# The first overflow job of a mixture-of-experts stage: its search and its loads moved into the fifth of eight passes

## The chip, the core and the metric

The kernel runs on one core of a Trainium2 chip. The core has a matrix engine (TensorE, PE in the profile), two engines for element-wise work that matter here (VectorE, DVE; ScalarE, ACT), a third one (GpSimd, POOL), and SyncE (SP), which in this kernel issues nearly all loads from device memory. ScalarE issues some loads too. Each engine takes its own instructions in the order in which they stand, and waits on semaphores for the others. The metric is the time of one execution in device microseconds, as the median over several runs.

## What is computed

Two blocks follow each other on 256 tokens of width 1024: a block with two attentions and a feed-forward network, and then two layers of the second kind, each with an attention, a mixture of experts and a gated per-layer embedding. The change is in the mixture of experts, once in each of the two layers (layer 0 and layer 1):

```
def hier_moe(xn, w_group, b_group, w_expert, b_expert, w_gate, w_up, w_down):
...
    e_w, e_idx = lax.top_k(e_prob, TOPK_IN_GROUP)
    e_w = e_w / jnp.sum(e_w, axis=-1, keepdims=True)
    comb = g_w * e_w
    expert_id = g_idx * EXPERTS_PER_GROUP + e_idx
    cw = jnp.einsum('tk,tke->te', comb, jax.nn.one_hot(expert_id, N_EXPERTS, dtype=jnp.float32)).astype(xt.dtype)
    hid = jax.nn.silu(jnp.einsum('td,edf->tef', xt, w_gate)) * jnp.einsum('td,edf->tef', xt, w_up)
    y = jnp.einsum('tef,efd->td', hid * cw[:, :, None], w_down)
```

There are 32 experts of width 128 in 4 groups; a token goes to two experts of one group. All is float32.

## The kernel before

The kernel computes an expert only for the tokens that chose it. It runs eight passes (`for q in range(8)`, L1129; the fifth has q = 4), each for four experts, and gives every expert 32 places (`CAP`). A pass runs, on PE: the gate and up matmuls of its four experts side by side (`gate_up`, L1021, L1027), the products of the pass before added into four accumulators (`combine`, L1054, L1058), a transpose of the hidden values (`turn`, L1038, L1040), the gather of tokens for later passes (`gather`, L983, L995) with the transposes of their choice (`slots`, L1008), and the down projection (`down`, L1043, L1047). Between them ScalarE and VectorE do the activation (`hidden`, L1032: tanh at L1034, then L1035 and L1036) and move results out of the accumulators (L1005, L1002, L1051, L1052). `turn` stands in PE's queue right behind `combine` and waits for the hidden values.

The weights of a pass are six tiles of 1 MB (four with gate and up of one expert, two with the down weights of two). A `Stream` takes them from a list and issues their loads on SyncE (L320, L328) into an arena of 21 tiles, as far ahead as `W.room(peak)` allows: at most 21 - peak tiles are held. The stage has `W.room(2)`, and from the sixth pass on `W.room(4)` in layer 1 and `W.room(9)` in layer 0.

An expert with more than 32 tokens is a job more. `jobs` (L953 to L957) counts these for each expert, `njob_i` is their number. They are run behind the last pass, by `overflow` (L1064): all engines read the number from memory into a register (L1068), skip the body if it is zero, and else run a loop. One trip of it loads a table of places (`place`, L1076), finds an expert with tokens left (L1078 to L1093), reads its number into a register of ScalarE (L1082), loads its three weights from there (L1084, L1085), makes the matrix that picks its tokens (L1095, L1096), gathers (L1104, whose matmuls are L995 too), and runs gate, up and down for up to 112 tokens (L1107 to L1124). Behind the branch comes the last pass's own `combine(T, True)` (L1177), and with it the end of the stage.

PE's and SyncE's instructions stand in the order of the code; those of the other engines are put in order by a scheduler.

Of the kernel before, what the change touches and what calls it, by code (L numbers as in the profile page):

```python
# [10 lines left out]
F32 = mybir.dt.float32  # L11
# [10 lines left out]
S = 256  # L22
# [229 lines left out]
def block_kernel(ctx, tc, I, out):  # L252
# [615 lines left out]
    def moe(l, router, rs):  # L868
# [195 lines left out]
        def overflow(T):  # L1064

            gu, dn = take("ovg", [2, 1024]), take("ovd", [1024])
            R = Step(new_d(128), T)
            n = nc.values_load(njob_i[0:1, 0:1], min_val=0, max_val=32)  # L1068
            with tc.If(n > 0):
                with tc.For_i(0, n, 1):  # L1070
                    tmp = sq2("job")
                    key, hot, cwh = tmp[:, 0:32], tmp[:, 32:64], tmp[:, 64:128].rearrange("p (t q e) -> p t q e", t=2, q=8)
                    top, cnt, keyj = tmp[:, 128:129], tmp[:, 129:130], tmp[:, 130:134].rearrange("p (t a) -> p t a", t=2)
                    wj, place, ei = tmp[:, 134:138].rearrange("p (t a) -> p t a", t=2), tmp[:, 256:384], tmp[:, 138:139]
                    wr = new_d(4)
                    nc.scalar.dma_start(place, I["c_place"])  # L1076
                    ebase = C("ebase")[:, 0:32]
                    V.tensor_scalar(key, ebase, float(S), None, OP.add)  # L1078
                    V.scalar_tensor_tensor(hot, jobs, 0.5, key, OP.is_gt, OP.mult)
                    V.tensor_reduce(top, hot, AX.X, OP.max)  # L1080
                    V.tensor_scalar(ei.bitcast(I32), top, 1.0 / S, -1.0, OP.mult, OP.add)
                    e = nc.values_load(ei.bitcast(I32)[0:1, 0:1], engines=(ENG.Activation,), min_val=0, max_val=31)  # L1082
                    for a, src in enumerate((I["moe_w_gate_2"], I["moe_w_up_2"])):
                        nc.scalar.dma_start(gu[:, a].unsqueeze(1), src[l, bass.ds(e, 1)].rearrange("e (p k) f -> p e (k f)", k=8))  # L1084
                    nc.scalar.dma_start(dn.unsqueeze(1), I["moe_w_down_2"][l, bass.ds(e, 1)].rearrange("e p n -> p e n"))  # L1085
                    V.tensor_scalar(hot, key, top, None, OP.is_equal)
                    V.tensor_tensor(key, jobs, hot, OP.mult)
                    V.tensor_reduce(cnt, key, AX.X, OP.add)
                    V.tensor_tensor(jobs, jobs, hot, OP.subtract)

                    V.tensor_scalar(cnt, cnt, float(MORE), float(CAP - MORE + 1 - S), OP.mult, OP.add)
                    V.tensor_tensor(cnt, cnt, top, OP.add)
                    V.tensor_scalar(keyj, k8[:, :, 0:2], cnt, None, OP.subtract)  # L1093
                    for t in range(2):
                        V.tensor_scalar(R.d[:, t], place, keyj[:, t, 0:1], None, OP.is_equal)  # L1095
                        V.scalar_tensor_tensor(R.d[:, t], place, keyj[:, t, 1:2], R.d[:, t].bitcast(F32),  # L1096
                                               OP.is_equal, OP.add)
                    for t in range(2):
                        V.tensor_tensor(cwh[:, t], cw[:, t, :, 0:4], hot.rearrange("p (q e) -> p q e", q=8), OP.mult)
                        V.tensor_reduce(wj[:, t, 0:1], cwh[:, t].rearrange("p q e -> p (q e)"), AX.X, OP.add)  # L1100
                        V.tensor_copy(wj[:, t, 1:2], cw[:, t, 0, 4:5])
                    A.copy(wr[:, :, 0:2], wj)
                    V.tensor_tensor(wr[:, :, 2:4], wj, wr[:, :, 0:2].bitcast(F32), OP.subtract)
                    drain(gather(R.d, [R], R.banks))  # L1104
                    b = R.bank("ex")
                    for t in range(2):
                        nc.tensor.transpose(b[:, t * 128:(t + 1) * 128], R.d[:, t].bitcast(F32), ident)  # L1107
                    for t in range(2):
                        mm(b[:, 256:260], R.d[:, t], wr[:, t], start=t == 0, stop=t == 1)
                    A.copy(R.d, b[:, 0:256].rearrange("p (t n) -> p t n", t=2))  # L1110
                    A.copy(R.ej[:, 0], b[:, 256:260])
                    V.tensor_tensor(R.cs, R.ej[:, 0, 0:2], R.ej[:, 0, 2:4], OP.add)
                    V.tensor_scalar(R.cs[:, 0:1], R.cs[:, 0:1], 0.5, None, OP.mult)
                    b = R.gu()
                    for k in range(8):
                        mm(b[:, 0:256], R.xe[:, k], gu[:, :, k * 128:(k + 1) * 128], start=k == 0, stop=k == 7)
                    hidden(R)
                    turn(R)
                    for c in range(2):
                        b = R.bank(f"y{c}")  # L1120
# [8 lines left out]
        for q in range(8):  # L1129
# [9 lines left out]
            if q == 2:  # L1139
                pv_ = ple_load(l)  # L1140
            if q == 5:
                W.room(4 if l else 9)
# [902 lines left out]
```

## Time and profile before

| | us |
|---|---|
| median of 3 runs | 880.39 (879.73 to 885.22) |
| the profiled execution | 883.1 |
| its span, first to last instruction | 881.3 |
| PE busy in the span | 829.3 (94%) |
| VectorE, ScalarE, GpSimd busy | 512.2, 453.0, 225.0 |
| mean granted clock of TensorE | 0.971 of full speed |

The rows below are from this one execution; times in them are microseconds from its first instruction unless marked ns. "ACTq" and "SPq" are the queues on which ScalarE and SyncE issue; a DMA row there gives the issue, not the transfer. The number in brackets is how long the engine idled before the instruction and whose work ended that. PEclk is the granted clock, where 1.00 is 2.4 GHz and 0.50 is 1.2 GHz. Matmul ends are modelled, so a row's length is that of a row of overlapping matmuls. In layer 0 the stage runs from about 484 to 626, in layer 1 from about 745 to 849.

### The profile page before, as it was taken

Reading aid. Unit: us, or ns where it says so; the run is one execution under the profiler, and the core shown is the slowest. Engines: PE = TensorE matmul, PEld = TensorE weight load, DVE = VectorE, ACT = ScalarE, POOL = GpSimd, SP = SyncE. Lnnn points to the kernel's source line nnn. Section 1 sums busy time; section 2 is a strip of 40 time slices with the busy share of each in tenths; the row PEclk is TensorE's granted clock in tenths of the full one; section 3 lists DMA queues with packets and bytes.
Section 4 is the critical chain, followed back from the end, with each engine's and each line's share of the span. In section 5 each row is a group of like instructions: output and inputs, shape, how many; then the busy total and the mean of one; then the engine's idle time right before and its main releaser. Section 6 shows DMA issues by size and latency. Waiting matters only on the chain. (4 is left out here: it accounts for less than half of the span.)

```text
span 881.3 us, 15729 instructions
## 1 busy us (share of the span) xinstructions
PE 829.3 (94%) x5660; PEld 647.4 (73%) x5660; DVE 512.2 (58%) x1479; ACT 453.0 (51%) x1106; POOL 225.0 (26%) x293
## 2 busy tenths in 40 slices
PE   8997999999999999999899999965899899999997
PEld 5995878999999988686667666635587778666656
DVE  5669656755454567678664544321688765543355
ACT  6675875544444456267675133420666774232463
POOL 2225542322222234214453200000122355000011
PEclk9998999999999999999799999995999899999999
DMA  9990429655556542446015699999463515799961
GB/s 307 385 375 31 146 81 399 237 191 171 198 179 188 182 144 96 161 141 237 1 50 197 254 378 406 408 397 379 157 207 129 208 66 193 293 384 406 408 262 49
DMA packets 85137, 200.05 MB, mean 227 GB/s; under 512 B 5776, under 2 KB 27584, under 8 KB 85056
## 3 DMA queue, kind: packets, MB, share of 16 engines
q1 hardware_dynamic: 82704, 195.61, 61.1%
q10 hardware_dynamic: 2352, 3.40, 1.1%
q8 instruction: 46, 0.75, 0.3%
q14 instruction: 35, 0.29, 0.1%
HBM read 197.93 MB, written 1.06 MB: 226 GB/s over the span
## 5 line engine op out<-in xcount | busy, mean ns | idle before, releaser
L537 DVE TENSOR_TENSOR s<-a,s 128x512 fp32r<-128x512 f32 (+3 forms) x281 | 189.5, 685 | 121.7 <-ACT s L536 87.0
L536 ACT CAST s<-a 128x512 fp32r<-128x512 f32 (+3 forms) x294 | 172.6, 600 | 169.8 <-PE pj L543 71.7
L541 PE MATMUL pj<-s,a 128*128 128x512 f32 (+3 forms) x456 | 176.1, 386 | 4.6 <-ACT a L518 3.0
L542 PE MATMUL pj<-s,a 128*128 128x512 f32 (+3 forms) x456 | 170.5, 374 | 5.9 <-DVE s L537 5.8
L543 PE MATMUL pj<-s,a 128*128 128x512 f32 (+3 forms) x456 | 170.4, 374 | 1.3 <-DVE a L519 1.2
L537 POOL TENSOR_TENSOR s<-a,s 128x512 fp32r<-128x512 f32 (+3 forms) x71 | 90.1, 1269 | 304.6 <-ACT s L536 246.6
L541 PEld LDWEIGHTS pj<-s,a 128*128 128x128 f32 x456 | 86.4, 190 | 24.1 <-issue 5.6
L534 POOL TENSOR_SCALAR s<-a 128x512 fp32r<-128x512 f32 (+3 forms) x58 | 40.3, 696 | 242.3 <-PE pj L543 113.9
L542 PEld LDWEIGHTS pj<-s,a 128*128 128x128 f32 x456 | 86.7, 190 | 20.1 <-DVE s L537 7.8
L543 PEld LDWEIGHTS pj<-s,a 128*128 128x128 f32 x456 | 86.6, 190 | 18.2 <-DVE a L519 3.6
L1517 PE MATMUL f<-a,s 128*128 128x256 f32 x256 | 72.6, 284 | 0.0
L1519 PE MATMUL f<-a,s 128*128 128x256 f32 x256 | 72.4, 283 | 0.0
L1518 PE MATMUL f<-a,s 128*128 128x256 f32 x256 | 72.4, 283 | 0.0
L1027 PE MATMUL gu<-a,xe 128*32 128x256 f32 x1024 | 58.7, 380 | 0.7 <-DVE xe L1002 0.7
L1027 PEld LDWEIGHTS gu<-a,xe 128*32 128x32 f32 x1024 | 32.5, 110 | 28.4 <-issue 4.9
L541 PE MATMUL acc<-s,a 128*128 128x512 f32 x128 | 50.1, 391 | 0.0
L542 PE MATMUL acc<-s,a 128*128 128x512 f32 x128 | 49.9, 390 | 0.0
L543 PE MATMUL acc<-s,a 128*128 128x512 f32 x128 | 49.8, 389 | 0.0
L1518 PEld LDWEIGHTS f<-a,s 128*128 128x128 f32 x256 | 49.1, 192 | 0.2
L1517 PEld LDWEIGHTS f<-a,s 128*128 128x128 f32 x256 | 49.1, 192 | 0.2
L1519 PEld LDWEIGHTS f<-a,s 128*128 128x128 f32 x256 | 49.1, 192 | 0.0
L638 POOL TENSOR_SCALAR P<-P,nd 128x128 f32<-128x128 f32 x64 | 30.2, 483 | 58.7 <-DVE nd L633 18.1
(365 smaller groups left out, 1426.1 us busy)
## 6 DMA issues: line engine op xcount, KB each, us to landing
a<-in_w_ff_dram SPq DMA_DIRECT2D x32, 1024.0 KB, 5.5
a<-in_moe_w_gate_dram SPq DMA_DIRECT2D x64, 512.0 KB, 6.8
a<-in_moe_w_up_dram SPq DMA_DIRECT2D x64, 512.0 KB, 7.5
a<-in_moe_w_down_dram SPq DMA_DIRECT2D x32, 1024.0 KB, 8.8
a<-in_a_w_in_dram SPq DMA_DIRECT2D x10, 1024.0 KB, 5.1
a<-in_ple_w_gate_dram SPq DMA_DIRECT2D x8, 1024.0 KB, 15.6
a<-in_w_in_dram SPq DMA_DIRECT2D x6, 1024.0 KB, 14.4
a<-in_w_o_dram SPq DMA_DIRECT2D x4, 1024.0 KB, 13.8
```

The costliest lines, as they stand in the source:

```text
L534: G.tensor_scalar(hi, wv, 1.0, 0.0, OP.mult, OP.add)
L536: A.copy(hi, wv)
L537: (G if nsplit[0] % 5 == 2 else V).tensor_tensor(lo, wv, hi.bitcast(F32), OP.subtract)
L541: mm(ps, xh, hi, start=st, stop=False)
L542: mm(ps, xh, lo, start=False, stop=False)
L543: mm(ps, xl, hi, start=False, stop=sp)
L638: G.tensor_scalar(p[:, o0:o0 + n], p[:, o0:o0 + n], rc[:, t, i:i + 1], 1.0, OP.mult, OP.mult)
L1027: mm(b[32 * e:32 * e + 32, 0:256], T.xe[:, k, 32 * e:32 * e + 32], w, start=k == 0, stop=k == 7)
L1517: mm(o, hi[:, fs], xt[0][:, k], start=st, stop=False)
L1518: mm(o, hi[:, fs], xt[1][:, k], start=False, stop=False)
L1519: mm(o, lo[:, fs], xt[0][:, k], start=False, stop=sp)
```

## The change

The function `overflow` becomes a class `Overflow`, whose parts are called at different places. At the top of the fifth pass (q = 4), in both layers: the table is loaded and the first expert is found (`__init__`, `find`), its weights are loaded (`load`), and all engines read the number of jobs. If there is no job, the expert's number is made to be the first one, so that the loads have a valid address. Behind the last pass: the choice of tokens (`pick`), and, if there is a job, gather, gate, up and down (`run`), then a loop over the jobs from the second on, whose trips do all steps. The small values lie in an arena tile of their own. The arena gets `W.room(4)` from the fourth pass on, and `W.room(6)` in layer 1 from the sixth.

```diff
-        def overflow(T):
-
-            gu, dn = take("ovg", [2, 1024]), take("ovd", [1024])
-            R = Step(new_d(128), T)
-            n = nc.values_load(njob_i[0:1, 0:1], min_val=0, max_val=32)
-            with tc.If(n > 0):
-                with tc.For_i(0, n, 1):
...
+        class Overflow:
...
+            def __init__(self):
+                self.gu, self.dn = take("ovg", [2, 1024]), take("ovd", [1024])
+                f = take("ovf", [512])
...
+                self.wr = tiny.tile([128, 2, 4], F32R, tag="wr", name="wr", bufs=1)
+                nc.scalar.dma_start(self.place, I["c_place"])
+                self.find()
+
+            def find(self):
+                key, hot, top, cnt, cwh, wj, wr = self.key, self.hot, self.top, self.cnt, self.cwh, self.wj, self.wr
+                V.tensor_scalar(key, C("ebase")[:, 0:32], float(S), None, OP.add)
+                V.scalar_tensor_tensor(hot, jobs, 0.5, key, OP.is_gt, OP.mult)
+                V.tensor_reduce(top, hot, AX.X, OP.max)
+
+                V.tensor_scalar(self.ei, top, 1.0 / S, 1.0, OP.mult, OP.max)
...
+                A.copy(wr[:, :, 0:2], wj)
+                V.tensor_tensor(wr[:, :, 2:4], wj, wr[:, :, 0:2].bitcast(F32), OP.subtract)
+
+            def load(self):
+                e = nc.values_load(self.ei[0:1, 0:1], engines=(ENG.Activation,), min_val=1, max_val=32) - 1
+                for a, src in enumerate((I["moe_w_gate_2"], I["moe_w_up_2"])):
+                    nc.scalar.dma_start(self.gu[:, a].unsqueeze(1),
+                                        src[l, bass.ds(e, 1)].rearrange("e (p k) f -> p e (k f)", k=8))
+                nc.scalar.dma_start(self.dn.unsqueeze(1), I["moe_w_down_2"][l, bass.ds(e, 1)].rearrange("e p n -> p e n"))
+
+            def pick(self, d):
+                for t in range(2):
+                    V.tensor_scalar(d[:, t], self.place, self.keyj[:, t, 0:1], None, OP.is_equal)
+                    V.scalar_tensor_tensor(d[:, t], self.place, self.keyj[:, t, 1:2], d[:, t].bitcast(F32),
+                                           OP.is_equal, OP.add)
+
+            def run(self, R):
+                drain(gather(R.d, [R], R.banks))
...
+                combine(R, False)
+
+            def all(self, T, n):
+                R = Step(new_d(128), T)
+                self.pick(R.d)
+                with tc.If(n > 0):
+                    self.run(R)
+                    with tc.For_i(1, n, 1):
+                        self.find()
+                        self.load()
+                        self.pick(R.d)
+                        self.run(R)
+                drop("ovg", "ovd", "ovf")
...
+            if q == 3:
+                W.room(4)
+            if q == 4:
+                over = Overflow()
+                over.load()
+                njob_r = nc.values_load(njob_i[0:1, 0:1], min_val=0, max_val=32)
             if q == 5:
-                W.room(4 if l else 9)
+                W.room(6 if l else 9)
...
-        overflow(T)
+        over.all(T, njob_r)
```

The first piece is ScalarE's queue in layer 0 between pass q=3 and pass q=4, in the kernel before. L1051 moves the last results of pass q=3 out, L1034 is the tanh of pass q=4.

```order
L1015 CAST d<-ex 128x2x128 [waits PE_49]
L1051 CAST yd<-y_5763 128x512 [waits PE_49,Activation_49]
L1051 CAST yd<-y_5771 128x512 [waits PE_49]
L1034 ACTIVATE hd<-gu,cs 128x128 [waits DVE_49,PE_49]
L1041 COPY hd<-ht 128x128 [waits PE_49]
```

The same place in the changed kernel; `a_5780` holds the small values, the table and the down weights, `a_5779` gate and up. Line numbers are those of the changed kernel from L1065 on.

```order
L1051 CAST yd<-y_5765 128x512 [waits PE_49]
L1079 DMA a_5780<-in_c_place_dram 128x128 [waits DMAHW1_49,DMAHW0_49]
L1105 TENSOR_LOAD a_5780 [waits DVE_49]
L1105 ISA x2
L1107 ISA
L1107 DMA a_5779<-in_moe_w_gate_dram 128x1024 [waits DMAHW7_49,DMAHW2_49]
L1101 CAST wr<-a_5780 128x2x2 [waits DVE_49]
L1107 ISA
L1107 DMA a_5779<-in_moe_w_up_dram 128x1024 [waits DMAHW4_49]
L1109 ISA
L1109 DMA a_5780<-in_moe_w_down_dram 128x1024 [waits DMAHW6_49]
L1034 ACTIVATE hd<-gu,cs 128x128 [waits PE_49]
```

Four loads, a register load and a cast now stand between the eviction and the tanh; layer 1 has the same rows.

The second piece is SyncE's queue in the changed kernel, in layer 0: the end of the loads for pass q=5 (`a_5604`, `a_5607` and `a_5610` are three of its experts, `a_5613` and `a_5692` its down weights), and the first load for pass q=6. `DMAHW0` to `DMAHW7` are eight completion counters; a load waits for the last load on the counter that it will use itself (where a row names PE too, for the buffer as well).

```order
L320 DMA a_5604<-in_moe_w_gate_dram 128x1024 [waits DMAHW7_49,PE_49]
L320 DMA a_5604<-in_moe_w_up_dram 128x1024 [waits DMAHW0_49]
L320 DMA a_5607<-in_moe_w_gate_dram 128x1024 [waits DMAHW1_49,PE_49]
L320 DMA a_5607<-in_moe_w_up_dram 128x1024 [waits DMAHW2_49]
L320 DMA a_5610<-in_moe_w_gate_dram 128x1024 [waits DMAHW3_49,PE_49]
L320 DMA a_5610<-in_moe_w_up_dram 128x1024 [waits DMAHW4_49]
L328 DMA a_5613<-in_moe_w_down_dram 128x2x1024 [waits DMAHW5_49,PE_49]
L328 DMA a_5692<-in_moe_w_down_dram 128x2x1024 [waits DMAHW6_49,PE_49]
L299 DMA a_5694<-in_ple_w_proj_dram 128x2x1024 [waits DMAHW7_49,PE_49]
L320 DMA a_5740<-in_moe_w_gate_dram 128x1024 [waits DMAHW1_49,PE_49]
```

Up to `a_5694` these rows are those of before; from there on the counters 0, 2, 4 and 6 of the next round are those of ScalarE's four loads.

The third piece is ScalarE's queue in the overflow branch of layer 0, before: what stands between the branch and the first move of gathered tokens (L1005).

```order
L1076 DMA job<-in_c_place_dram 128x128 [waits DMAHW0_49]
L1082 TENSOR_LOAD job [waits DVE_49]
L1082 ISA x2
L1084 ISA
L1084 DMA a_6266<-in_moe_w_gate_dram 128x1024 [waits DMAHW3_49,DMAHW2_49,DMAHW1_49]
L1084 ISA
L1084 DMA a_6266<-in_moe_w_up_dram 128x1024 [waits DMAHW2_49]
L1085 ISA
L1085 DMA a_6267<-in_moe_w_down_dram 128x1024 [waits DMAHW5_49,DMAHW4_49,DMAHW3_49]
L1102 CAST d<-job 128x2x2 [waits DVE_49,Activation_49]
L1005 ACTIVATE xe<-ov,small 128x128 [waits DVE_49]
```

And now:

```order
L1171 TENSOR_LOAD stage
L1143 COMPARE_AND_BRANCH
L1005 ACTIVATE xe<-ov,small 128x128 [waits DVE_49]
L1005 ACTIVATE xe<-ov,small 128x128
L1124 CAST d<-ov 128x256 [waits PE_49]
L1005 ACTIVATE xe<-ov,small 128x128 [waits DVE_49]
```

The loads, the register load of the expert's number and the cast are gone from there.

## Rows read from the trace of the kernel before

**Rows 1.** The page: busy us (share of the span) and instructions of each engine

```profile
PE 829.3 (94%) x5660; PEld 647.4 (73%) x5660; DVE 512.2 (58%) x1479; ACT 453.0 (51%) x1106; POOL 225.0 (26%) x293
```

**Rows 2.** Timeline, layer 0's branch: start us, us, engine, line, operation, [idle before <- releaser]

```profile
587.06 1.92 PE L1047 MATMUL y<-a,hd 128*32 128x512 f32 x16 [0.35 <-ACT hd L1041]
...
590.82 0.18 DVE L1078 TENSOR_SCALAR job<-cst 128x32 f32<-128x32 f32 x1 [0.46 <-DVE yd L1052]
...
598.57 0.34 ACTq L1076 DMA_DIRECT2D job<-in_c_place_dram  x1
...
603.95 0.48 DVE L1095 TENSOR_SCALAR d<-job 128x128 fp32r<-128x128 f32 x2 [10.92 <-DMA job<-in_c_place_dram]
...
604.84 7.06 PE L995 MATMUL ov<-d,a 128*128 128x128 f32 x32 [15.85 <-DVE d L1096]
...
608.69 0.20 ACT L1102 CAST d<-job 128x4 fp32r<-128x4 f32 x1 [19.05 <-DMA a<-in_b_w_q_dram]
...
612.42 5.06 PE L1116 MATMUL ov<-a,xe 128*128 128x256 f32 x16
...
621.20 2.39 PE L1058 MATMUL acc<-yd,d 128*128 128x512 f32 x8
...
624.33 2.11 PE L1058 MATMUL acc<-yd,d 128*128 128x512 f32 x8 [0.73 <-PE acc L1058]
```

**Rows 3.** DMA issues, 538.3 to 539: count, KB each, us from issue to landing

```profile
a<-in_moe_w_down_dram SPq DMA_DIRECT2D x1, 1024.0 KB, 13.0
```

**Rows 4.** Timeline of SyncE's issues, layer 0

```profile
537.87 1.10 SPq L328 DMA_DIRECT2D a<-in_moe_w_down_dram  x2
...
551.68 0.33 SPq L320 DMA_DIRECT2D a<-in_moe_w_gate_dram  x1
```

**Rows 5.** Stretches, layer 0: length, busy by engine (x), PEclk, DMA share, GB/s

```profile
548.00:560.00 12.00, 12.00 (x131) 8.78 (x131) 3.56 (x11) 3.85 (x11) 0.00 (x0) 1.00 1.03 407
```

**Rows 6.** Stretches, PE alone: length, PE busy (x), PEclk, DMA share, GB/s

```profile
588.99:604.84 15.85, 0.00 (x1) 0.57 1.05 385
604.00:614.00 10.00, 9.16 (x40) 0.50 1.06 376
614.00:616.00 2.00, 2.00 (x8) 0.70 1.09 377
```

**Rows 7.** Timeline of PE, layer 0, passes q=4 and q=6

```profile
546.42 0.27 PE L1040 MATMUL ht<-ident_r,hd 128*128 128x128 f32 x1
546.44 3.77 PE L995 MATMUL g<-d,a 128*128 128x128 f32 x32
...
573.49 3.66 PE L1027 MATMUL gu<-a,xe 128*32 128x256 f32 x64
578.52 0.30 PE L1040 MATMUL ht<-ident_r,hd 128*128 128x128 f32 x1 [1.37 <-DVE hd L1036]
```

**Rows 8.** DMA issues from ScalarE, 480 to 640: count, KB each, us to landing

```profile
a<-in_moe_w_gate_dram ACTq DMA_DIRECT2D x1, 512.0 KB, 6.4
...
job<-in_c_place_dram ACTq DMA_DIRECT2D x1, 64.0 KB, 5.3
```

**Rows 9.** Timeline of ScalarE, layer 0, passes q=4 and q=6

```profile
544.67 0.37 ACT L1034 ACTIVATE hd<-gu,cs 128x128 f32<-128x128 f32 x1 [2.92 <-PE gu L1027]
...
577.30 0.37 ACT L1034 ACTIVATE hd<-gu,cs 128x128 f32<-128x128 f32 x1 [3.11 <-PE gu L1027]
```

**Rows 10.** Timelines of PE and SyncE, layer 1

```profile
804.31 0.27 PE L1040 MATMUL ht<-ident_r,hd 128*128 128x128 f32 x1
...
809.33 0.33 SPq L320 DMA_DIRECT2D a<-in_moe_w_gate_dram  x1
```

**Rows 11.** Timeline of PE's weight loads, layer 1, start of pass q=7

```profile
838.39 0.13 PEld L1027 LDWEIGHTS gu<-a,xe 128*32 128x32 f32 x4 [0.30 <-DMA a<-in_moe_w_down_dram]
```

**Rows 12.** One line's instructions, layer 1: xcount, ns min/median/max, first and last start

```profile
L1069 PEldq COMPARE_BRANCH  x1: 232/232/232, 845.5 to 845.5; - x1
L1069 PEldq EVENT_SEMAPHORE  x1: 51/51/51, 847.0 to 847.0; - x1
```

More of the change, by code (lines that the diff above doesn't have):

```diff
@@ L1062, in combine @@
                         (A.copy if t else V.tensor_copy)(h[:, t, c * 512:(c + 1) * 512], acc[t][c])
-        def overflow(T):
-            gu, dn = take("ovg", [2, 1024]), take("ovd", [1024])
-            R = Step(new_d(128), T)
-            n = nc.values_load(njob_i[0:1, 0:1], min_val=0, max_val=32)
-            with tc.If(n > 0):
-                with tc.For_i(0, n, 1):
[L1071 to L1120, printed above, removed]
-                        mm(b, R.hT, dn[:, c * 512:(c + 1) * 512], start=True, stop=True)
-                        A.copy(R.yd[c][:, 0], b)
-                        V.tensor_tensor(R.yd[c][:, 1], b, R.yd[c][:, 0].bitcast(F32), OP.subtract)
-                    combine(R, False)
-            drop("ovg", "ovd")
```

36 lines of the change are left out of this document (added).

## The prediction

> **What bounds the kernel now.** I read the page's busy shares first: TensorE (PE) works 829.3 of 881.3 us [rows 1], so time is lost only where its queue, which runs strictly in order, stands still. The timeline shows the one long pause, in the overflow branch of layer 0 [rows 2]. The last down projection of the passes ends at 587.06 + 1.92 = 588.98, and the branch's gather starts at 604.84, after 15.85 us of idling. Follow the rows backwards. The gather waits for VectorE's choice of rows (L1095), that waits for the table `place`, and ScalarE issues this load (L1076) only at 598.57. ScalarE is then held to 608.69, when its cast of two columns runs after 19.05 us of idling, though VectorE had its input ready long before (its search starts at 590.82 and is over by 603.95 - 10.92 = 593.03). So a load on ScalarE's queue holds everything behind it on that engine.
>
> Why are those loads late? The order's second piece names eight completion counters, 0 to 7, which the loads use in turn: a load waits for the last one on its counter, so it goes out when the one eight before it has landed. In layer 0 the second down load of pass q=5 leaves at about 538.6 (second of the pair at 537.87) and lands 13.0 us later, at 551.6 [rows 3]; the eighth load behind it leaves at 551.68 [rows 4]. The DMA engines are full in this stretch (share 1.03, 407 GB/s [rows 5]).
>
> The clock is the second cost of a pause. Over the idle stretch the granted clock is 0.57 on average, hence mostly 0.50 (the 1.2 GHz level); 0.50 stays while PE already works again, through 604 to 614, and 614 to 616 has 0.70 [rows 6], so it returns about 10.4 us after PE restarts. In these the gather takes 7.06 us and the gate and up matmuls 5.06 [rows 2]; the same gather at full clock takes 3.77 and a pass's gate and up matmuls 3.66 [rows 7]. The loss is (7.06 - 3.77) + (5.06 - 3.66) = 4.7 us.
>
> Layer 1 has no overflow: the instructions of the branch body stand in the trace once, in layer 0.
>
> **What the change takes away.** In layer 0 the table, the choice of rows and the weights are in place before the branch, so the gather can follow the last down projection. The pause of 15.85 us and the slow clock behind it, 4.7 us, go: -20.55 us, of 624.33 - 588.98 = 35.35 from the last down projection to the final combine. What is left of it, 14.8, is the branch's own chain. The least it can save is the pause alone, 15.85.
>
> **What it adds, by each queue that the step is moved past.** Four loads and a register load now stand on ScalarE between pass q=3's second eviction and pass q=4's tanh (the order's first piece), in both layers, whether there is an overflow or not. Their waits are those of the counters:
> - `place` waits for counter 0, gate for 2, up for 4, down for 6. By SyncE's rows (the order's second piece) these belong to pass q=5's second and third up loads, fourth up load and second down load. The last of these is what holds ScalarE: 551.7 by the trace of before.
> - The three loads ahead of it on ScalarE's own queue (64 + 512 + 512 KB) share the DMA engines with it. Before, such a gate load took 6.4 us from issue to landing, `place` 5.3 [rows 8]. None of them ahead of the down load would add 0, all of them 1.11 MB at 407 GB/s = 2.7 us. I take 2.2, since the gate load, out at about 544, lands near 550.5, and the up load only overlaps the rest: 553.9.
> - Then comes the issue (0.35) and a gap of 0.1, so the tanh starts at 554.3 where it started at 544.67 [rows 9]. From tanh to the transpose that PE waits for is 578.52 - 577.30 = 1.22 [rows 7, 9]: the transpose runs at 555.5 instead of 546.42 [rows 7]. **A pause of 9.1 us** (bounds 6.9 to 9.6). Behind the transpose in PE's queue stand the gather for pass q=5, the down projection and all that follows, so nothing fills it.
> - Layer 1 repeats it. The eighth load behind the second down load goes out at 809.33, so: 809.3 + 2.2 + 0.45 + 1.22 = 813.2 against 804.31 [rows 10]. **8.9 us** (6.7 to 9.4).
> - Either pause is far longer than the 2 to 3 us after which the clock fell in the idle stretch (0.57 over 15.85 us means 0.50 from about 2.2 us on). The work after it begins with the same gather of 32 matmuls that restarted at half clock in the branch. So 4.7 us again, **twice**. Bounds: 0, if the clock returns at once, and 3.77 + 1.92 + 3.66 = 9.4, if all of the gather, the down projection [rows 2] and the next pass's gate and up matmuls runs at half clock.
>
> A rule of the Trainium skill bears on the 2.2: "DMA: Bandwidth & Descriptors", section "Queues, rings and completion order", says that a DMA engine goes round the queues that have work, packet by packet. By it ScalarE's loads get their share at once, the full 2.7 us would lie ahead of the down load, and the sum would be 1 us longer.
>
> **What costs nothing, and what hides it.** The search's some 18 VectorE instructions (2.2 us before) run while VectorE would wait for the held tanh; without that cover they would cost those 2 us per layer. The register loads of the job count move off the end of the stage to pass q=4, where PE's queue runs ahead of its array. The choice of rows (four VectorE instructions) falls under pass q=7's combine. The prefetch has two tiles fewer, but in these passes SyncE's loads leave as earlier ones land, not as tiles come free. In layer 1 the loads bring 1.64 MB that nobody uses, 4.0 us of a full DMA. It would fall on pass q=7, whose weights arrive just in time (PE idles 0.30 for them at 838.39 [rows 11]), but PE comes there 13 us later than before, so the weights are early.
>
> The loop over further jobs (n = 1: no trip) is jumped over; before, its end was a meeting of all engines, 0.74 us from the last matmul's end (621.20 + 2.39) to 624.33 [rows 2]. In layer 1 PE's branch past the body (845.5 to 845.7) is followed by its next step at 847.0, part of which is a wait for ScalarE [rows 12], so a jump costs 0 to 1.3 us. I take 0.7: nothing changes.
>
> **Sum.** 9.1 + 8.9 + 2 x 4.7 - 20.55 = **+6.9 us** on 883.1, the profiled execution's time, 890.0. This execution lies 2.7 above the median of the three runs (880.4), so I forecast **887.3** for the median, 0.8% slower. Less than 1% (8.8 us) is what a measurement of this kernel hardly tells from no change.
>
> **The rivals.**
> - A, slower: the clock stays low through the whole of what follows each new pause, up to the next pass's gate and up matmuls, since the gather and the small transposes keep PE less full. For: in the branch it came back only after the gather was over, inside the wide matmuls. Against: the down projection, wide too, comes before them. Price 2 x (9.4 - 4.7) = 9.4: 896.7. It passes 1% when the loss is above 5.7 per layer.
> - B, level: the clock returns within some 3 us of restart. For: here PE pauses 9 us and not 16. Against: the same gather restarts it. 18.0 + 2 x 1.5 - 20.55 = +0.5: 880.9.
> - C, faster: ScalarE is not held, because the counters are free when it comes. Against: SyncE's own loads wait for the same counters to the tenth of a microsecond. Then only the bytes count, 4.0 us before pass q=7 in each layer: 8.0 - 20.55 = -12.5: 867.9.
> - D, slower: the jump past the loop body waits for code. "Runtime: NRT & Kernel Launch", section "Instruction fetch mechanics", says that a taken branch to a page outside the buffer forces a DMA fetch. Row-wise: the nearest price of a small transfer under full queues is the 5.3 us of `place` [rows 8], less the 0.7 taken: 891.9. The 0 to 1.3 of layer 1 speaks against it.
>
> **How the numbers follow.** Forecast 0.55, with its own range 883 to 892 from the stall's bounds (13.6 to 19.0 instead of 18.0) and 1.5 of clock on either side; about a fifth of it lies above 889.2. A 0.20, B 0.12, C 0.08, D 0.05. Slower by over 1%: 0.2 x 0.55 + 0.20 + 0.05 = 0.36. Faster by over 1%: C, 0.08. Within 1%: 0.56. The range takes in B with its lower stall bound (880.9 - 3) and A nearly to its price: 878 to 896; C and the far end of A, some 0.13, are left out.
>
> **What would show it.** In the trace of after: PE's transpose L1040 of pass q=4 waits 8 to 10 us in both layers, with ScalarE's loads of L1107 and L1109 going out at about 547 and 554 (layer 0), and the granted clock at 0.50 for some 10 us behind it. The gather of the branch follows the last L1047 within 1 us, and the final combine within 14 to 16 us. If the transpose does not wait, C holds and the forecast is wrong by 20 us; if it waits and the clock stays at 1.00, B.

## The result, and the profile after

The changed kernel takes 895.31 us (median of 4 runs, 891.15 to 896.64); the kernel before took 880.37 us in its 4 runs beside it. The ratio is 1.0144 (95% interval 1.0106 to 1.0182): slower by more than 1%. The forecast was 887.3 us; 895.3 lies near the upper end of the range of 878 to 896. The profiled execution took 891.15 us, with a span of 889.3 us. It is the shortest of the four.

TensorE works as long as before (829.3 us there, [rows 1]), so again everything is in its waits.

```profile
PE 829.5 (93%) x5660; PEld 647.6 (73%) x5660; DVE 515.4 (58%) x1501; ACT 453.7 (51%) x1107; POOL 226.2 (25%) x293
```

**The new pause in layer 0.** The timelines of TensorE and of ScalarE with its DMA issues (ACTq), pass q=4; columns: start, length, engine, line, operation, [idle before <- what ended it]:

```profile
540.11 2.12 PE L1058 MATMUL acc<-yd,d 128*128 128x512 f32 x8
553.41 0.45 PE L1040 MATMUL ht<-ident_r,hd 128*128 128x128 f32 x1 [11.18 <-DVE hd L1036]
553.51 7.07 PE L995 MATMUL g<-d,a 128*128 128x128 f32 x32
...
561.18 3.64 PE L1047 MATMUL y<-a,hd 128*32 128x512 f32 x16
564.59 3.73 PE L1027 MATMUL gu<-a,xe 128*32 128x256 f32 x64
```

```profile
539.67 0.36 ACTq L1107 DMA_DIRECT2D a<-in_moe_w_gate_dram  x1
...
543.98 0.35 ACTq L1107 DMA_DIRECT2D a<-in_moe_w_up_dram  x1
551.66 0.34 ACTq L1109 DMA_DIRECT2D a<-in_moe_w_down_dram  x1
552.05 0.37 ACT L1034 ACTIVATE hd<-gu,cs 128x128 f32<-128x128 f32 x1 [11.78 <-DMA a<-in_moe_w_down_dram]
```

The tanh (L1034) stands behind three weight loads, and the last goes out only at 551.66. TensorE waits 11.18 us, and then works at half clock: the gather takes 7.07 us where it took 3.77 [rows 7], the down projection 3.64 where it took 1.92.

**The same in layer 1**, TensorE:

```profile
796.24 2.12 PE L1058 MATMUL acc<-yd,d 128*128 128x512 f32 x8
807.91 0.45 PE L1040 MATMUL ht<-ident_r,hd 128*128 128x128 f32 x1 [9.55 <-DVE hd L1036]
...
818.24 3.63 PE L1027 MATMUL gu<-a,xe 128*32 128x256 f32 x64
```

In the kernel before, the same stretches, from that combine to the next pass's gate and up multiplications (layer 0, then layer 1), were 7.79 us each:

```profile
544.46 2.12 PE L1058 MATMUL acc<-yd,d 128*128 128x512 f32 x8
...
552.25 3.64 PE L1027 MATMUL gu<-a,xe 128*32 128x256 f32 x64
```

```profile
802.35 2.12 PE L1058 MATMUL acc<-yd,d 128*128 128x512 f32 x8
...
810.14 3.64 PE L1027 MATMUL gu<-a,xe 128*32 128x256 f32 x64
```

They are now 564.59 - 540.11 = 24.48 and 818.24 - 796.24 = 22.00: **+16.7 us and +14.2 us**.

**The branch of layer 0** after, TensorE:

```profile
599.51 1.92 PE L1047 MATMUL y<-a,hd 128*32 128x512 f32 x16 [0.35 <-ACT hd L1041]
601.36 3.79 PE L995 MATMUL ov<-d,a 128*128 128x128 f32 x32
...
605.37 3.70 PE L1130 MATMUL ov<-a,xe 128*128 128x256 f32 x16
...
612.78 2.39 PE L1058 MATMUL acc<-yd,d 128*128 128x512 f32 x8
620.02 3.78 PE L1058 MATMUL acc<-yd,d 128*128 128x512 f32 x8 [4.85 <-DMA a<-in_b_w_out_dram]
...
625.22 0.80 PE L541 MATMUL pj<-s,a 128*128 128x512 f32 x1
```

The pause of 15.85 us [rows 2] is gone, and the gather and the gate and up multiplications run at full clock. But ahead of the final combine stands a **new wait of 4.85 us**. From the last down projection to the final combine it was 624.33 - 587.06 = 37.27 us [rows 2]; it is 620.02 - 599.51 = 20.51: **-16.8 us**, not -20.55.

**What the new wait is.** The waits by line, 612 to 621 us:

```profile
POOL s L534 <- DMA a<-in_b_w_out_dram: 39.3, 1, 39.3
...
ACT s L536 <- DMA a<-in_b_w_out_dram: 6.3, 1, 6.3
...
PE acc L1058 <- DMA a<-in_b_w_out_dram: 4.8, 1, 4.8
```

Three engines are set free by one DMA, which none of their next instructions reads. The rows of line 1145, the loop over the second and later jobs, show why. In two narrow windows (616.4 to 617 and 619.1 to 619.2) each of the five engines has one semaphore event, all at the same moment. Of each window, SyncE's and TensorE's row (xcount, ns min/median/max, first and last start):

```profile
L1145 SPq EVENT_SEMAPHORE  x1: 28/28/28, 616.5 to 616.5; - x1
...
L1145 PEldq EVENT_SEMAPHORE  x1: 51/51/51, 616.5 to 616.5; - x1
```

```profile
L1145 SPq EVENT_SEMAPHORE  x1: 27/27/27, 619.1 to 619.1; - x1
...
L1145 PEldq EVENT_SEMAPHORE  x1: 51/51/51, 619.2 to 619.2; - x1
```

These are semaphore events of the program at the loop's line. They fall together with the landings of the two one-megabyte loads of output weights that SyncE had issued last ahead of the loop: the first went out at 603.3 and landed 13.3 us later, and for the second the trace gives no landing of its own, but at 619.1 the DMA engines have fallen silent: the rate over 608 to 622 (40 slices of 0.35 us) goes to 0 just there and comes back only when SyncE, itself held at the loop, issues the next:

```profile
GB/s 328 336 342 345 345 351 357 357 372 366 372 372 392 383 375 404 380 374 386 380 404 398 298 217 135 123 129 41 23 23 12 0 0 0 0 0 23 47 146 123
```

So the trace suggests that at this loop's edge every engine waits for every load in flight, even when the loop makes no trip. The experiments below test that.

**The account.** Between the two profiled executions:

| stretch | forecast, us | measured, us |
|---|---|---|
| layer 0, pass q=4: pause and slow clock | +13.8 | +16.7 |
| layer 1, pass q=4: pause and slow clock | +13.6 | +14.2 |
| layer 0, last down projection to final combine | -20.55 | -16.8 |
| final combine to the next projection (625.22 - 620.02, before 628.88 - 624.33) | 0 | +0.65 |
| everything else | 0 | -6.8 |
| sum (span 889.3 - 881.3) | +6.9 | +8.0 |

The first four make +14.8 us, about the difference of the medians (14.9). "Everything else" is the clock in code that the change does not touch. The larger part, one stretch of before, then of after (length, busy time by engine, granted clock, DMA share, GB/s):

```profile
430.00:440.00 10.00, 10.00 (x60) 7.15 (x60) 5.44 (x26) 3.43 (x13) 1.83 (x5) 0.61 0.01 2
```

```profile
430.00:440.00 10.00, 10.00 (x91) 6.64 (x92) 8.71 (x45) 7.62 (x30) 4.59 (x11) 1.00 0.01 3
```

The profiled execution of after escaped most of a stretch at the lower clock in the attention and came to the experts 4.34 us earlier (first gather at 493.14, 497.48 before). The other 2.45 us lie in the attention ahead of layer 1's experts: before ran 693 to 701 at a mean granted clock of 0.57, after stayed at 1.00 there. The other three runs of after, 894.6 to 896.6, presumably escaped less; their mean granted clock of 0.962 to 0.966 against 0.969 fits that, but they have no trace, so this stays an inference.

### The profile page after: what moved, and what is told of

Its sections match the earlier page's. It is cut to its first block, busy times and chain, and to the rows that moved or that the text cites. A ratio compares the mean times of both kernels' runs of the same rounds, so it can differ in the third digit from the quotient of the medians.

```text
span 889.3 us, 15756 instructions
## 1 busy us (share of the span) xinstructions
PE 829.5 (93%) x5660; PEld 647.6 (73%) x5660; DVE 515.4 (58%) x1501; ACT 453.7 (51%) x1107; POOL 226.2 (25%) x293
## 5 line engine op out<-in xcount | busy, mean ns | idle before, releaser
L995 PEld LDWEIGHTS g<-d,a 128*128 128x128 f32 x320 | 44.9, 219 | 4.4 <-DVE d L937 2.4
```

The source lines that it names most:

```text
L995: mm(b[:, i * n:(i + 1) * n], hr[hl][:, t, (m * j + i) * 128:(m * j + i) * 128 + 128], d[:, t], start=t + i + hl == 0, stop=t + i + hl == ...
```

## The experiments

Ten kernels ran. Each time stands beside runs of the kernel before on the same chip.

| run | edit | median, us | ratio to before (95%) |
|---|---|---|---|
| changed kernel | | 895.31 | 1.0144 (1.0106 to 1.0182) |
| e1 | early loads issued by SyncE | 880.54 | 0.9996 (0.9977 to 1.0015) |
| e2 | early in layer 0 only | 878.79 | 0.9980 (0.9956 to 1.0004) |
| e3 | loop inside a branch | 888.23 | 1.0067 (1.0040 to 1.0094) |
| e5 | pause filled with work | 890.02 | 1.0084 (1.0053 to 1.0114) |
| e6 | e1 and e3 together | 871.89 | 0.9870 (0.9834 to 0.9906) |
| e7 | six loads held back behind the loop | 887.74 | 1.0088 (1.0061 to 1.0115) |
| e8 | e6 in layer 0, layer 1 as before | 867.38 | 0.9859 (0.9835 to 0.9884) |
| e9 | e8 with layer 1 early too | 870.21 | 0.9884 (0.9863 to 0.9906) |
| e10 | e8 with six loads held back | 864.85 | 0.9817 (0.9788 to 0.9845) |
| e11 | kernel before with six loads held back | 872.14 | 0.9901 (0.9863 to 0.9938) |

### e1: the early loads on SyncE's queue

```diff
-                e = nc.values_load(self.ei[0:1, 0:1], engines=(ENG.Activation,), min_val=1, max_val=32) - 1
+                e = nc.values_load(self.ei[0:1, 0:1], engines=(ENG.SP,), min_val=1, max_val=32) - 1
-                    nc.scalar.dma_start(self.gu[:, a].unsqueeze(1), ...
+                    nc.sync.dma_start(self.gu[:, a].unsqueeze(1), ...
-                nc.scalar.dma_start(self.dn.unsqueeze(1), ...
+                nc.sync.dma_start(self.dn.unsqueeze(1), ...
```

> The changed kernel with one edit: the first expert's number is read and its three weight loads are issued by SyncE, the queue that streams all other weights, instead of ScalarE. Theory S (ScalarE's tanh stands behind loads that wait for completion counters, and nothing else makes the new pause): the wait at the transpose of pass q=4 falls from 11.2 us (layer 0) and 9.6 us (layer 1) to under 2 us in both, the clock stays at its full level behind it, and the 16.5 us of layer 0 and 13.2 us of layer 1 that the changed kernel's trace shows there are given back: 895.3 - 29.7 = 865.6 us, 862 to 872 us with what the meeting at the loop's edge costs when the branch comes earlier. Rival B (the 1.64 MB of loads themselves delay the weights of passes 5 to 7 on a link that is already busy at a share of 1.02): the wait moves from the transpose to the first gate and up multiplication of pass 5 or 6, 4 to 8 us per layer, and the time stays at 880 to 888 us.

Measured: 880.54 us, no difference from the kernel before. Theory S is right on the pause and wrong on the time. TensorE, layer 0:

```profile
539.83 2.12 PE L1058 MATMUL acc<-yd,d 128*128 128x512 f32 x8
541.79 0.27 PE L1040 MATMUL ht<-ident_r,hd 128*128 128x128 f32 x1
...
579.53 3.61 PE L1027 MATMUL gu<-a,xe 128*32 128x256 f32 x58 [1.96 <-DMA a<-in_moe_w_up_dram]
...
598.93 2.38 PE L1058 MATMUL acc<-yd,d 128*128 128x512 f32 x8
618.41 3.78 PE L1058 MATMUL acc<-yd,d 128*128 128x512 f32 x8 [17.10 <-DMA a<-in_b_w_out_dram]
```

The transpose follows without a wait, so ScalarE's place behind its own loads made the pause. Rival B's wait is there too, but small: 1.96 us for late weights, whether by the 1.64 MB or by the two tiles fewer of prefetch this run can't tell (e9 can, for layer 1). The gain went elsewhere. TensorE ends the branch at 601.3 and then stands **17.10 us** at the loop's edge, until the same load as before has landed: 618.4 here, 620.0 in the changed kernel. Whatever TensorE saves in layer 0 ahead of that point is taken back there.

### e2: early in layer 0 only

```diff
-                over = Overflow()
-                over.load()
+                over = None if l else Overflow()
+                if not l:
+                    over.load()
 ...
-        over.all(T, njob_r)
+        if l:
+            late_branch(T, njob_r)      # find, load and run inside the branch, as before
+        else:
+            over.all(T, njob_r)
```

> The changed kernel, but layer 1 finds and loads its expert inside the branch as the kernel before does; layer 0 is as changed. Theory S: layer 1, where no expert has a job, loses its pause of 9.6 us and the slow clock behind it, 9.2 + 4.1 = 13.2 us by the two traces, and nothing of layer 0 moves: 895.3 - 13.2 = 882 us (880 to 884). Rival (the pause in layer 1 only takes the place of waits for weights further on, so that part of it is given back later): 886 to 892 us.

Measured: 878.79 us. The theory's direction holds (layer 1's pause is gone and nothing takes its place; the rival's 886 to 892 is out). The number is 1.2 us below the expected range: the price of layer 1 in medians is 895.3 - 878.8 = 16.5 us, 14.2 by the two traces. The rest is about what the stretch at the lower clock makes between executions, and stays open. The verdict on layer 0 is the weightier one: moving the search and loads there, alone, is worth nothing that can be told from no change. Its wait at the loop's edge is longer, 5.79 us, because TensorE came 1.9 us earlier (this execution's pause in pass q=4 was 10.02 us) and the load landed only 1.0 earlier:

```profile
619.05 3.78 PE L1058 MATMUL acc<-yd,d 128*128 128x512 f32 x8 [5.79 <-DMA a<-in_b_w_out_dram]
```

### e3: the loop entered only with more than one job

```diff
-                    with tc.For_i(1, n, 1):
-                        self.find()
+                    with tc.If(n > 1):
+                        with tc.For_i(1, n, 1):
+                            self.find()
 ...
```

> The changed kernel with the loop over the second and later jobs put inside a branch of its own that is entered only with more than one job, so that with one job no engine comes to the loop's edge. Theory M (at the loop's edge all five engines wait for every load in flight, the last one megabyte of the attention output weights landing at 619.13 us of the changed kernel's trace): the wait of 4.85 us ahead of the final combine falls to under 1.5 us, and with the slow clock behind it 4.1 + 0.7 = 4.8 us are given back: 890.5 us (889 to 892). Rival F (the wait is the fetch of code behind a taken jump over the loop's body): the jump is still taken over the same body, the wait stays near 4.8 us and the time at 895 us.

Measured: 888.23 us, somewhat under the 889 to 892 of theory M. The decisive row is the wait:

```profile
615.24 2.39 PE L1058 MATMUL acc<-yd,d 128*128 128x512 f32 x8
618.11 2.11 PE L1058 MATMUL acc<-yd,d 128*128 128x512 f32 x8 [0.48 <-PEq L1145]
```

The jump over the same body is still taken, and costs 0.48 us; the clock stays up too (2.11 us, where the changed kernel's final combine took 3.78). So it was not code fetch (rival F, and rival D of the prediction). The page "Runtime: NRT & Kernel Launch" of the Trainium skill (section "Instruction fetch mechanics") says that a taken branch to code outside the buffer stalls the engine for a fetch. Whether this jump's target lies outside it no run shows; above these 0.48 us there is no such stall here.

### e5: the pause filled with work

```diff
             b = T.bank("ht")
+            if fill:
+                warm(fill, b)      # 40 in pass q=4: products of constants, overwritten by the transpose
             nc.tensor.transpose(b[:, 0:128], T.hd, ident)
```

> The changed kernel with 40 multiplications of constants (128x512, bf16, 0.22 us each, into the bank that the transpose overwrites) ahead of the transpose of pass q=4 in both layers: they use nothing and nobody reads them, they only keep TensorE at work for 8.9 us of the pause. Theory C (the slow clock behind the pause is a price of standing idle, and apart from the pause itself): the transpose starts as late as in the changed kernel, within 0.5 us, but the granted clock stays at 1.00 behind it, the next 32 gather multiplications take 3.8 us instead of 7.1, and 4.9 + 4.1 = 9.0 us are given back: 886.3 us (885 to 888). Rival (the clock falls for another reason, such as the number of engines and transfers at work together): 895 us or, where the filling outlasts the pause, up to 897.

Measured: 890.02 us against the expected 886.3. The clock does what theory C says; TensorE, layer 0 (line 1042 is the transpose here, and 1060 the combine):

```profile
543.46 8.81 PE L378 MATMUL ht<-ones_b 128*128 128x512 bf16 x40
553.18 0.33 PE L1042 MATMUL ht<-ident_r,hd 128*128 128x128 f32 x1 [0.91 <-DVE hd L1036]
553.26 3.77 PE L995 MATMUL g<-d,a 128*128 128x128 f32 x32
...
620.00 3.78 PE L1060 MATMUL acc<-yd,d 128*128 128x512 f32 x8 [10.40 <-DMA a<-in_b_w_out_dram]
```

The transpose is as late as before, and the gather behind it takes 3.77 us. But the final combine starts at 620.00, as in the changed kernel (620.02): layer 0's 4.9 us went into the wait at the loop's edge, now 10.40 us. Only layer 1's part (4.1 to 4.5 by the traces) is left; 895.3 - 890.0 = 5.3.

### e6: both edits

The edits of e1 and e3 in one kernel.

> The changed kernel with both edits: the first expert's loads issued by SyncE, and the loop over later jobs inside a branch that is entered only with more than one job. With the loads on SyncE alone the branch began 17.3 us earlier than in the kernel before, and 17.1 us of that were lost again where TensorE stood at the loop's edge until the last load in flight had landed (618.3 us). Theory M (all engines wait there for the loads in flight, and nobody else needs them so early): the final combine follows the branch within 1.5 us, and most of the 17.1 us and the slow clock behind it (3.5 us) come off 880.5: 860 to 866 us. Rival N (the stage behind the branch needs the same loads, so that the wait only moves to its first projections): 872 to 881 us.

Measured: 871.89 us, between the two theories and the first version faster than the kernel before. The final combine follows the branch within 0.42 us, as M says; then a part of N comes. ScalarE, behind the branch:

```profile
614.21 0.47 ACT L518 ACTIVATE a<-tps,small 128x256 fp32r<-128x256 f32 x1 [3.57 <-SPq L1145]
```

TensorE's first projection waits 4.18 us for it. ScalarE waits not for a transfer but until SyncE itself, still issuing the loads ahead in its queue, has come past line 1145.

### e7: the loop as it is, six loads fewer in flight

```diff
             if q == 5:
                 W.room(6 if l else 9)
+            if q == 7 and not l:
+                W.room(NB)         # the stream of weights stops here
 ...
         over.all(T, njob_r)
+        if not l:
+            W.room(9)              # and goes on here
```

> The changed kernel with its loop as it is, but six of the twelve one-megabyte loads for the attention behind (two of its query weights, two of its key and value weights, two of its output weights) are issued behind the loop of layer 0 instead of ahead of it: the stream of weights stops in pass 7 and goes on behind the branch. Theory M (at the loop's edge all engines wait for the loads in flight): six loads less at about 2.6 us each have long landed when TensorE comes, so the wait of 4.85 us ahead of the final combine falls under 1.5 us; what the attention then waits for its own late weights comes on top and is not of this theory (0 to 15 us), so the total says little: 888 to 905 us. Rival F (code fetch behind the taken jump, with a link that is now empty): the wait stays at 3 us or more.

Measured: 887.74 us, just under the expected 888 to 905, and 7.6 below the changed kernel. The same loop, the same jump, fewer loads:

```profile
611.09 2.39 PE L1058 MATMUL acc<-yd,d 128*128 128x512 f32 x8
615.02 2.14 PE L1058 MATMUL acc<-yd,d 128*128 128x512 f32 x8 [1.55 <-POOL s L534]
```

The wait is 1.55 us, at the edge of what M allowed (1.5), and no DMA ends it: from 602 to 612 the DMA engines are all but silent (share 0.01), so nothing was left in flight when TensorE came. The final combine starts 5.0 us earlier than in the changed kernel (615.02, with the pass's own pause 1.4 us shorter). The attention did not wait for its late weights: the first projection comes at 618.29, after 0.26 us of idling. Holding the loads was free.

### e8 and e9: the best of these, with and without layer 1

e8: layer 0 loads early through SyncE; the loop is behind a branch of its own and its loads are on ScalarE; layer 1 searches and loads inside its branch.

```diff
-            def load(self):
-                e = nc.values_load(self.ei[0:1, 0:1], engines=(ENG.Activation,), min_val=1, max_val=32) - 1
+            def load(self, eng=None, kind=ENG.Activation):
+                eng = eng or nc.scalar
+                e = nc.values_load(self.ei[0:1, 0:1], engines=(kind,), min_val=1, max_val=32) - 1
 ...
-                over = Overflow()
-                over.load()
+                over = None if l else Overflow()
+                if not l:
+                    over.load(nc.sync, ENG.SP)
```

> Layer 0 as in the run with both edits (first expert's loads issued early by SyncE, loop over later jobs behind a branch of its own), but the loads inside that loop are issued by ScalarE, so that no later stage has to wait until SyncE, late in its own queue, has come past the loop; layer 1 finds and loads inside its branch, as the kernel before. In the run with both edits ScalarE waited 3.6 us at L518 behind the branch for SyncE's row at L1145, and the clock fell behind that. If that wait goes too, layer 0 keeps the 17.7 us by which TensorE was ahead of the kernel before at the branch's transpose, and layer 1 keeps the time of before: 880.4 - 17.7 = 862.7 us, 860 to 865. If ScalarE waits there for another reason (the output weights in flight, or the buffer), layer 0 keeps 14.2 us: 866 to 868 us.

Measured: 867.38 us. The first reason given was wrong: with the loop's loads on ScalarE, ScalarE still waits for SyncE to pass:

```profile
610.01 0.47 ACT L518 ACTIVATE a<-tps,small 128x256 fp32r<-128x256 f32 x1 [2.65 <-SPq L1146]
```

What at that line ScalarE needs of SyncE the trace doesn't say, and it was not tried further. e9 is e8 with layer 1 early too:

> As the run before, but layer 1 too finds and loads its expert early through SyncE, 1.64 MB that no job uses. By the rows of the run with both edits layer 1 lost 2.6 us to the first gate and up multiplications of pass 5 and 6, which waited for their weights behind these loads, and 1.9 us to a slow clock: 2.6 to 4.5 us over the run before. If useless loads were free, the two would be within 1 us of each other.

Measured: 870.21 us, 2.8 us over e8, within the expected 2.6 to 4.5. The two intervals overlap a little. The useless 1.64 MB are not free: in layer 1 TensorE waits for its own weights, which it does not in e8, whose prefetch is the same:

```profile
822.00 3.61 PE L1027 MATMUL gu<-a,xe 128*32 128x256 f32 x58 [1.95 <-DMA a<-in_moe_w_up_dram]
```

### e10 and e11: holding the loads, with the early search and without

e10 adds the edit of e7 to e8, e11 adds it to the kernel before, and does nothing else.

> The run with layer 0 on SyncE, the loop behind a branch of its own and layer 1 as before, and in addition the six loads for the attention held back behind the branch. In the run without that, ScalarE waited 2.7 us and TensorE 3.3 us behind the branch because SyncE, in order of its own queue, came to the branch only at 610 us, behind ten one-megabyte loads; the clock fell for 3.4 us behind that. With six loads less ahead of it SyncE comes past before TensorE does: the 3.3 us and 1.7 us of slow clock go, 867.4 - 5 = 862.4 us (860 to 865). If the attention then waits for its late weights instead: 866 us or more.

> The kernel before, with only the six loads for the attention held back behind the branch of layer 0. The branch there waits 15.85 us for its search, its table of places and a link full of other loads, and its end stands at the loop's edge with the last load at 622.1 us, 0.7 us ahead of TensorE. If the full link makes a large part of the branch's wait, the table lands in 2 to 3 us instead of 5.3 and the wait falls by 3 to 5 us: 875 to 878 us. If holding the loads is by itself worth nothing there (the wait is search and issue), the time stays at 880 us, and what the last two runs gained is not the holding.

e10: 864.85 us, the fastest version, 1.8% faster than the kernel before. ScalarE's wait for SyncE is gone; the first projection comes after 0.51 us:

```profile
612.22 0.50 PE L541 MATMUL pj<-s,a 128*128 128x512 f32 x1 [0.51 <-ACT a L518]
```

Its interval overlaps that of e8, so the step from e8 to e10 is shown by the row and only made likely by the time.

e11: 872.14 us, more than was expected of it (875 to 878). TensorE in the branch:

```profile
597.04 7.06 PE L995 MATMUL ov<-d,a 128*128 128x128 f32 x32 [7.29 <-DVE d L1096]
```

The pause that the change was to remove falls from 15.85 to 7.29 us with nothing moved but six loads of someone else. What shrank is ScalarE's wait to send the table's load out, whose only wait in the order's third piece is counter 0:

```profile
590.78 0.34 ACTq L1076 DMA_DIRECT2D job<-in_c_place_dram  x1
```

That is 1.03 us after the end of the last down projection (589.75 here); before it was 598.57 - 588.98 = 9.59 us [rows 2], until a load of query weights that SyncE had sent out at 584.3 landed 14.2 us later. The difference is the whole gain of 8.56 us. The reason given in the expectation, a faster landing, did not come: the table still took 5.3 us, on a link as full as before (383 GB/s from 590 to 596). So over half of the pause was the completion counter behind other loads, not the search. The unmoved search with this one edit beats the moved one by 2.4% (0.9901 against 1.0144). Moving it is still worth something in e10, with its other edits: 864.85 against 872.14, and the two intervals do not meet.

## Why the prediction was right or wrong

**The saving in the branch** (-20.55) was right as far as it was described: pause and slow clock are gone, 37.27 - 20.51 = 16.8 us net, and with the 4.1 us by which the wait at its end grew (4.85 instead of 0.73, [rows 2]) that is 20.9.

**The step that failed** is "The loop over further jobs (n = 1: no trip) is jumped over ... nothing changes." I had seen the meeting of all engines at the loop's end and read it as a price of 0.74 us. It ends when the last load in flight has landed; with nothing in flight it cost 0.73 to 1.55 us (before, e7). In the kernel before, the last load and TensorE came within 0.7 us of each other. SyncE and TensorE at line 1070, the loop there (SyncE has stood there since 613.1 and is past its last load at 622.2, where the first of its two rows begins; TensorE arrives at 622.9):

```profile
L1070 PEldq COMPARE_BRANCH  x1: 80/80/80, 622.9 to 622.9; - x1
...
L1070 SPq EVENT_SEMAPHORE  x2: 658/718/777, 622.2 to 622.9; - x2
```

So behind the 20.55 us there was hardly any slack. The link is full through layer 0's passes, before (share 1.03 in [rows 5]) as after (stretches: the last two columns are DMA share and GB/s):

```profile
520.00:540.00 20.00, 19.98 (x232) 13.12 (x222) 9.29 (x41) 6.77 (x18) 0.00 (x0) 1.00 1.03 409
...
580.00:600.00 20.00, 18.26 (x190) 11.15 (x194) 5.08 (x15) 5.79 (x12) 0.81 (x1) 1.00 1.04 390
600.00:612.00 12.00, 10.39 (x72) 7.85 (x65) 3.19 (x8) 3.38 (x10) 0.00 (x0) 1.00 1.07 368
```

The same loads pass ahead of the loop in both kernels, and layer 0 cannot end before them. From the first gather to the final combine the changed kernel takes 620.02 - 493.14 = 126.88 us, the kernel before 624.33 - 497.48 = 126.85: layer 0 gained nothing with its new pause, and without it, in e1, 1.3 us (618.41 - 492.82 = 125.59).

**The pauses in pass q=4** were right in place, cause and the clock behind them. Layer 1 was sized within 0.6 us (14.2 for 13.6). Layer 0 came out at 16.7 for 13.8, and its pause of 11.18 us lies above the bounds of 6.9 to 9.6. The term that was too small is the 2.2 us by which ScalarE's own loads hold back the down load that frees them. In the changed kernel's trace TensorE came there 4.35 us earlier (540.11 against 544.46), and the down load too left 4.0 us earlier (second of the pair that begins at 533.88; in [rows 4] the pair begins at 537.87), but it landed at the same 551.7. SyncE's issue, and the time to landing of the second of the pair:

```profile
533.88 1.09 SPq L328 DMA_DIRECT2D a<-in_moe_w_down_dram  x2
```

```profile
a<-in_moe_w_down_dram SPq DMA_DIRECT2D x1, 1024.0 KB, 17.1
```

It took 17.1 us where it took 13.0 [rows 3]: 4.1 and not 2.2. In layer 1 it took 15.5 where it took 12.9: 2.6. In both layers all 1.11 MB of ScalarE's three loads came through ahead of its landing, so the 2.7 that the prediction had as its upper bound, and as what the rule beside it would give, was right; in layer 0 half a megabyte more of SyncE's own came through too (5.8 MB against 5.3, both at 406 to 407 GB/s), the other 1.3 us. Why, no run shows. That the transpose ran at 553.4, ahead of my 555.5, is only the 4.3 us by which this execution came earlier. e1 confirms the cause, e5 the clock: the pauses cost 5.4 and 4.5 us more than the 11.3 and 9.7 by which they delay the transpose.

**The rivals.** A (clock low through the next gate and up multiplications): no, these took 3.73 and 3.63 us, at full clock. B and C: no; ScalarE was held and the clock fell. But C's picture, ScalarE not held, was made in e1, and its 867.9 did not come: 880.5, for the loop's edge. D had the right place (the branch's end) and nearly the size (5.3; measured 4.85) by the wrong mechanism, and 0.05 for it was too little for what it stood for.

**The sum.** 887.3 missed 895.3 by 8.0 us: 2.9 for layer 0's pause, 0.6 for layer 1's, 3.8 for the branch's end, 0.65 for the slow clock behind it. The range of 878 to 896 held by luck: its upper end had been made for rival A, which did not come, and the wait at the loop's edge was in no term. The forecast's own range of 883 to 892 did not hold 895.3, and it doesn't follow from the bounds named beside it either: 4.4 us down and 1.0 up for the stall, with 1.5 for the clock, make 881.4 to 889.8.

## What to carry to other kernels

Before you count a saving, ask what ends the next meeting point, and how much slack lies behind the work you shorten: a loop that makes no trip can make every engine wait for every load in flight, and then the DMA stream sets the time, not the engine you freed. Put loads that must wait for a completion counter on a queue that does nothing else; a compute engine that issues them stands behind them with all its work. Where a load can't go out because its completion counter waits for others' loads, first try to let those go later: here that alone gained 1%, and moving the search gained only once that, or the loop's edge, was dealt with.

## What the runs showed of the hardware

- At the edge of a loop that makes no trip TensorE stood until the last load in flight had landed: 4.85, 5.79, 10.40 and 17.10 us in four kernels that reached it at different times, and all four went on at 618.4 to 620.0. The waits are semaphore events that the program has at the loop's line, on all five engines, and so come with how the loop is written. With the loop behind a branch the same place cost 0.48 us.
- A 1 MB load with 1.11 MB from another engine's queue beside it landed after 17.1 us instead of 13.0 (layer 0) and after 15.5 instead of 12.9 (layer 1), on a link at 406 to 408 GB/s throughout.
- A pause of 9 to 11 us brought the granted clock to 0.50, and 40 small constant products in the pause kept it at 1.00; the gather behind took 3.77 instead of 7.07 us.
- A stretch of the attention that no edit touches ran 430 to 440 us at a mean clock of 0.61 in one profiled execution and at 1.00 in another, worth some 4 us in the time.
